# Four changes of order in a two-layer mixer and FFN trunk: splits of block sums, turns of the values, PSUM-emptying steps, and four gate pairs

## The chip, the core and the metric

The kernel runs on one core of a Trainium2 chip. The metric is the device time of one execution in microseconds (us). Engines are named as the profile does: PE (TensorE matmuls, PEld its weight loads), DVE (VectorE), ACT (ScalarE), POOL (GpSimd), SP (SyncE, which here only issues DMAs).

## What is computed

Two layers on x of 1024 tokens by 1024, all in float32. Each layer norms x, projects it with one matrix w_in (1024 by 5120) to queries, keys and values of two attentions and to two gates, runs both attentions, joins them by the gates, projects with w_o and adds to x. A gated FFN with a short convolution follows. The part of the reference that matters here:

```python
proj = h @ w_in[l]
qa, ka, va, qb, kb, vb, gate_pre = jnp.split(proj, splits, axis=-1)
o_a = dilated_mixture(hd4(qa, DSW_HEADS), hd4(ka, DSW_HEADS), hd4(va, DSW_HEADS))
o_b = stick_breaking_attention(hd4(qb, SB_HEADS), hd4(kb, SB_HEADS), hd4(vb, SB_HEADS))
gates = jax.nn.sigmoid(gate_pre + b_gate[l])
merged = g_a * (o_a @ w_br[l, :OUT_A]) + g_b * (o_b @ w_br[l, OUT_A:])
x = x + merged @ w_o[l]
```

The dilated mixture has three groups of four heads with dilations 1, 4 and 16; the stick-breaking attention has four heads.

## The kernel before

**Numbers.** Each float32 operand is split into a high and a low part of type fp32r (`split`, L142 and L147: a cast on ACT, then a subtraction on DVE), and a product is three matmuls: high by high, high by low and low by high.

**A layer's mixer.** `head(l)` first projects the values (`v_ps`) and the keys and queries (`kq_ps`, `q_ps`) of the first heads of the stick-breaking attention. Each PSUM bank is emptied by a step on ACT and one on DVE (L557 and L558 for values, L582/L583 and L579/L580 for keys and queries in `in_parts`), and the parts go to DRAM.

The rest of the input projection is a list of work that the class `Dense` hands out in *shares* (a share is six matmuls of 128x512 in the products of pairs). There are four plain gates (`gate`, tile `g_ps`), and then *pairs*: two column blocks of w_in at once, by seven products in place of eight (Strassen's method, function `pair`, L1055 to L1120). The products are gathered in PSUM banks `i_a`, `i_c`, `i_a`, `i_c`, `i_a`, `i_b`, `i_a`; each is emptied by a step of ACT or DVE (L1087, 1091, 1094, 1100, 1105, 1112, and the last in `put`, L1119). A pair is 14 shares. The right-hand sides include sums of blocks of h: S[1] to S[4], built by `block_sums` (L980 on): sums on POOL (L990, 995, 996, tile `h_sum`, three instructions each), and splits of these into `t_hi` on ACT and `t_lo` on DVE by `in_two`. S[3], the first series of sums, is read by the fifth product of a pair. `series` hands the steps out one at a time while the head's products run (`dense.aside`).

Pairs are of four kinds: `pair_near` (keys and queries of near heads), `pair_v` (values, which are transposed by PE in `turn` (`v_t`, L1161) into a buffer `vv` and written to DRAM as `tv`), `pair_kq` (keys and queries of the far groups, written to DRAM as `tk0` and `tk1` for the two pairs of heads, L1134), and `pair_gate`. Before, a layer's order (`dense.main`, then `dense.seven`) is: near 2, v 0, near 4, near 6, v 1, kq 1 0, kq 2 0, v 2, kq 1 1, kq 2 1, and then the six gate pairs 2 to 7.

**Attention between the shares.** `attend` writes the items of both attentions between the shares: 16 stick items (B), 4 near items (N) and 16 far items (T00 to T07 for `tk0`, T10 to T17 for `tk1`). A far item fetches keys and queries from DRAM (`fetch_kq`, L834, tile `t_kq`, 768 KB), computes scores `z` (L621, L622) at least LEAD_T = 3 shares later, transposes (`t`, L881 to L883), splits (`p1h`, `p1l`) and applies them (`o`, L891, L893). Fetches of T1x need the pairs kq 1 1 and kq 2 1 done, those of T0x kq 1 0 and kq 2 0. A first stick item has a mask on DVE (L685), a scan, and an output `sb_o` (L725) of the split `sbl`.

**What sets the order.** PE's order is that of the code. The order on ACT, DVE and POOL is the Tile scheduler's, which goes by its model of the times, by priorities, and by dependencies added by hand; `tc.high_priority(offset=AHEAD)` with AHEAD = 200 puts a step ahead of others, and a NO_SYNC dependency orders two instructions of one engine without a semaphore. SP issues DMAs in program order, and an issue that has to wait for its data holds up those behind it.

Of the kernel before, what the change touches and what calls it, by code (L numbers as in the profile page):

```python
# [12 lines left out]
ALU = mybir.AluOpType  # L13
# [6 lines left out]
KD = D // P  # L20
# [7 lines left out]
SCALE = 0.125  # L28
# [16 lines left out]
RATE_N = 0.75  # L45
RATE_T = 0.5
PLAIN = 4
LEAD = 6
LEAD_N = 7
LEAD_T = 3  # L50
# [2 lines left out]
AHEAD = 200  # L53
# [3 lines left out]
def f32(ap):  # L57
    return ap.bitcast(F32)
# [3 lines left out]
def trunk_kernel(ctx, tc, x, norm1, w_in, b_gate, w_br, w_o, norm2, w_up, conv_w, conv_b, w_down, norm_f, out, depth=None, probe=None):  # L62
# [23 lines left out]
    LAST = {}  # L86
# [49 lines left out]
        return sb.tile([P, 2048 // c, c], dtype, tag="xa", bufs=4, name=name)  # L136


    def split(hi, lo, src, turn=None):


        one = act.copy(hi, src)  # L142
        if turn == "is":
            LAST["act"] = one.ins.name
        elif turn == "waits" and "act" in LAST:
            tc.add_manual_dep(one.ins, LAST["act"], NO_SYNC, reason="in turn")
        two = dve.tensor_tensor(lo, src, f32(hi), ALU.subtract)  # L147
        if turn == "is":
            LAST["dve"] = two.ins.name
        return two  # L150
# [390 lines left out]
    def values_part(vt, w, ms):  # L541
        for m in ms:
            o = bank("ps", "v_ps")
            for j in range(2):
                t = 2 * m + j
                n, c = t // 4, t % 4
                tok = slice(c * P, (c + 1) * P)
                pairs = []
                for k in range(KD):
                    hh, hl = h_part(n, k)  # L550
                    pairs.append(((hh[:, tok], hl[:, tok]), w[k]))
                yield from product(o[:, j * 256 : (j + 1) * 256], pairs)
                if j == 0:
                    yield
            ov = o.rearrange("p (j h c) -> p j h c", j=2, h=4)
            vv = vt[m // 2][:, 2 * (m % 2) : 2 * (m % 2) + 2, :, :]
            act.copy(vv[:, :, :, 0:64], ov)  # L557
            dve.tensor_tensor(vv[:, :, :, 64:128], ov, f32(vv[:, :, :, 0:64]), ALU.subtract)  # L558
# [17 lines left out]

    def in_parts(c, scale, hi, lo, x):
        if c:
            act.mul(hi, x, scale)  # L579
            dve.scalar_tensor_tensor(lo, x, scale, f32(hi), ALU.mult, ALU.subtract)  # L580
        else:
            act.copy(hi, x)  # L582
            dve.tensor_tensor(lo, x, f32(hi), ALU.subtract)  # L583

    def kq_half(c, w, n):
        o = bank("ps", "kq_ps"[c:])
        yield from product(o, [(w[k], h_part(n, k)) for k in range(KD)])
        hi, lo = small("kq_h", F32R), small("kq_l", F32R)
        in_parts(c, SCALE, hi, lo, o)
        keep_kq(c, n, 0, hi, lo)  # L590
        yield

# [387 lines left out]
    def block_sums(more):  # L980


        last, rs = {}, {}

        def first(t, a, b, i):
            if i == 0:
                new_s(t)
                rs[t] = quarter("h_sum") if t == 3 else sb.tile([P, 4, HF], F32, tag="ql", bufs=2, name="h_sum")
            r, (ah, al), (bh, bl) = rs[t][:, i, :], a()[i], b()[i]
            one = pool.tensor_tensor(r, f32(al), f32(bl), ALU.subtract)  # L990
            if last:
# [4 lines left out]
            last["sum"] = pool.tensor_tensor(r, r, f32(bh), ALU.subtract).ins.name  # L996

        def second(i):
            if i == 0:
                new_s(2)  # L1000
            in_two(1, i)
            r, (ah, al) = rs[1][:, i, :], b22()[i]
            dve.tensor_tensor(r, f32(ah), r, ALU.subtract)
            dve.tensor_tensor(r, r, f32(al), ALU.add)

        def fourth(i):
            if i == 0:
                S[4] = half(0, 0)
            r, (ah, al) = small("h_sum"), b21()[i]
            dve.tensor_tensor(r, f32(ah), f32(S[2][i][0]), ALU.subtract)  # L1010
            dve.tensor_tensor(r, r, f32(S[2][i][1]), ALU.subtract)
            dve.tensor_tensor(r, r, f32(al), ALU.add)
            split(*S[4][i], r, "waits")

        def in_two(t, i):
            split(*S[t][i], rs[3 if t == 3 else 1][:, i, :], "waits")

        b11, b12, b21, b22 = (lambda n=n, k=k: half(n, k) for k in range(2) for n in (1, 0))
        todo = []

        def series(after, lag, gap, f, g):

            at = {}
            for i in range(4):
                at.setdefault(i * gap, []).append(lambda i=i: f(i))
                at.setdefault(i * gap + lag, []).append(lambda i=i: g(i))
            for k in range(3 * gap + lag + 1):
                todo.append((after, lambda fs=at.get(k, ()): [h() for h in fs]))

        series(set(), 3, 2, lambda i: first(3, b22, b12, i), lambda i: in_two(3, i))  # L1030
        series({"head"}, 3, 2, lambda i: first(1, b12, b11, i), second)
        for i in range(4):
# [15 lines left out]
    def pair(dense, l, offs, tiled, put):  # L1048
# [35 lines left out]
        pa, pc = bank("ps", "i_a"), bank("ps", "i_c")  # L1084
        yield from seven(pa, w1, half(1, 0), True, True)
        yield
        act.copy(view(u1), grid(pa))  # L1087
        w7 = piece(u2, "waits")
        yield from seven(pc, w5, S[1], True, True)
        yield  # L1090
        act.copy(view(u5), grid(pc))
        w2 = piece(a12)
        yield from seven(pa, w6, S[2], False, True)
        act.copy(view(u2), grid(pa))
# [5 lines left out]
        dve.tensor_tensor(view(u2), view(u2), grid(pc), ALU.add)  # L1100
# [4 lines left out]
        dve.tensor_tensor(view(u5), view(u5), grid(pa), ALU.add)  # L1105
# [6 lines left out]
        dve.tensor_tensor(view(u1), view(u1), grid(pb), ALU.add)  # L1112
        put(0, 1, u1, False, a12)
        yield
        yield "turn"
        for word in seven(pa, w4, S[4], False, True):
            yield
            yield "turn"
        put(1, 1, grid(pa), True)  # L1119
        yield  # L1120

    def pair_kq(dense, l, g, pr):
# [32 lines left out]
    def pair_v(dense, l, g):  # L1155


        def turn(c, n, f):
            tp = bank("s", "v_t")
            for r in range(4):  # L1160
                pe.transpose(tp[:, r * P : (r + 1) * P], f[:, r * P : (r + 1) * P], ident)  # L1161
            tw = tp.rearrange("p (r h c) -> p r h c", r=4, h=2)
            vv = sb.tile([P, 4, 2, P], F32R, tag="ot", name="vv")
            with tc.high_priority(offset=AHEAD):
                act.copy(vv[:, :, :, 0:64], tw)
                dve.tensor_tensor(vv[:, :, :, 64:128], tw, f32(vv[:, :, :, 0:64]), ALU.subtract)
            for h in range(2):
                if g:
                    there = tv[c][h, :, :, g - 1, n * P : (n + 1) * P].rearrange("r p c -> p r c")
                else:  # L1170
                    there = sv[4 + 2 * c + h][:, 4 * n : 4 * n + 4, :]
                nc.sync.dma_start(there, f32(vv[:, :, h, :]))
            if (c, n) == (1, 1):
                dense.done |= {f"v{g}"} if g else {f"V{u}" for u in range(4, 8)}

        def put(c, n, x, psum, room=None):
            f = x
            if psum:
                f = small("vf")
                act.copy(f.rearrange("p (r j) -> p r j", r=4) if g else f, x)  # L1180
            dense.at(3, lambda: turn(c, n, f))

        off = OFF_VA + 256 * g
        return pair(dense, l, (off, off + P), g > 0, put)
# [34 lines left out]
    def mixer(l, pending):  # L1219
# [1 line left out]
        vectors = setup(l)  # L1221
        dense = Dense()
        dense.plain = [gate(l, c) for c in range(PLAIN)]
        dense.seven = [pair_gate(dense, l, e) for e in range(PLAIN // 2, KD)]
        dense.side = block_sums([(set(), zeros)] * (l == 0))
        dense.done |= {"K0", "K1", "V0", "V1", "V2", "V3"}
        if l:
# [25 lines left out]
        for _ in vectors:  # L1253
            pass
        dense.main = [
            *((None, set(), f, True) for f in (pair_near(dense, l, 2), pair_v(dense, l, 0), pair_near(dense, l, 4), pair_near(dense, l, 6))),
            *((None, set(), f, True) for f in (pair_v(dense, l, 1), pair_kq(dense, l, 1, 0), pair_kq(dense, l, 2, 0))),
            *((None, set(), f, True) for f in (pair_v(dense, l, 2), pair_kq(dense, l, 1, 1), pair_kq(dense, l, 2, 1))),
        ]
# [816 lines left out]
```

## Times and profile before

| what | value |
|---|---|
| median of 3 runs | 2702.91 us (2699.21 to 2703.39) |
| profiled execution | 2701.9 us, span 2700.0 us |
| mean granted clock of PE | 0.992 |
| PE busy | 2635.3 us, 98% of the span |
| DVE, ACT, POOL busy | 2084.5, 1342.1, 673.6 us |

One execution was profiled; rows give start and duration in us. In a wait row, "A <- B: s, n, m" says that A's engine was idle n times before it, s us together and m at most, and that B ended this. Rows with `xN` group N instructions. Issues on SP are told apart from the landing of the DMA they start, which the page lists as "DMA to landing".

### The profile page before, as it was taken

The page shows a single profiled execution, that of the slowest core. Times are in us where ns is not written, and L with a number is a line of the kernel's source. Part 1 is how long each engine was busy: PE and PEld are TensorE (multiplying, and loading weights), DVE is VectorE, ACT ScalarE, POOL GpSimd, SP SyncE. Part 2 cuts the span into 40 slices and gives each one's busy share as a digit, 9 for nine tenths or more (in the row PEclk, how much of TensorE's full clock was granted, in tenths as well). Part 3 has the DMA queues.
Part 4 walks back from the last instruction along what each step waited for, and adds up shares of the span by engine and source line. Part 5 has one row for each costly group of instructions (what it writes and reads, how often), then busy time and mean ns, then how long its engine had stood idle before and what let it go on. Part 6 is the DMA issues. An engine that isn't in the chain of part 4 may idle for free.

```text
span 2700.0 us, 36777 instructions
## 1 busy us (share of the span) xinstructions
PE 2635.3 (98%) x12780; PEld 2201.9 (82%) x12780; DVE 2084.5 (77%) x3159; ACT 1342.1 (50%) x2488; POOL 673.6 (25%) x483
## 2 busy tenths in 40 slices
PE   8899999999999999999989999999999999999999
PEld 7778788888888888888877787888888888888888
DVE  5687776786789888897657778667858888988865
ACT  5355555565555555432334555655745545454225
POOL 5200011112224433321161011010321443343210
PEclk9999999999999999999999999999999999999999
DMA  6546566674335443588443565856732444446863
GB/s 214 171 131 172 152 189 195 220 257 134 90 117 170 139 160 136 214 326 313 173 117 115 154 161 153 234 191 211 265 87 78 154 158 138 167 144 254 328 251 122
DMA packets 418917, 482.94 MB, mean 179 GB/s; under 512 B 26420, under 2 KB 336044, under 8 KB 416940
## 3 DMA queue, kind: packets, MB, share of 16 engines
q1 hardware_dynamic: 418716, 480.59, 55.4%
q8 instruction: 101, 1.65, 0.3%
q14 instruction: 84, 0.69, 0.1%
q10 hardware_dynamic: 16, 0.00, 0.0%
HBM read 307.43 MB, written 173.08 MB: 178 GB/s over the span
## 4 chain that ended last, share of the span: by engine, by line
PE 81%; DVE 9%; ACT 2%; DMA 2%; issue 2%; POOL 1%; SPq 0%; DVEq 0%; ACTq 0%; POOLq 0%
PE u_a L974 5%; PE u_a L975 5%; PE u_a L976 5%; PE d_ps L1704 4%; PE d_ps L1705 4%; PE d_ps L1706 4%; PE i_a L974 3%; PE i_a L976 3%; PE i_a L975 3%; PE u_c L974 3%; PE u_c L976 3%; PE u_c L975 3%; PE o_ps L179 2%; PE o_ps L181 2%; PE o_ps L180 2%; PE i_c L974 2%
## 5 line engine op out<-in xcount | busy, mean ns | idle before, releaser
L147 DVE TENSOR_TENSOR w_lo<-up_a,w_hi 128x512 fp32r<-128x512 f32 x240 | 237.5, 996 | 20.7 <-ACT w_hi L142 20.7
L142 ACT CAST w_hi<-up_a 128x512 fp32r<-128x512 f32 x240 | 149.4, 622 | 184.4 <-PE u_a L975 45.3
L1070 POOL TENSOR_TENSOR u<-in_a 128x512 f32<-128x512 f32 x32 | 45.2, 1412 | 767.0 <-DMA in_a<-in_w_in_dram 232.8
L1712 DVE TENSOR_TENSOR x<-x,d_ps 128x512 f32<-128x512 f32 (+1 forms) x228 | 152.1, 671 | 78.0 <-PE d_ps L1706 76.9
L1443 POOL TENSOR_TENSOR cv<-cv 128x512 f32<-128x512 f32 x88 | 132.3, 1516 | 249.2 <-DVE cv L1438 126.3
L142 ACT CAST w_hi<-in_a 128x512 fp32r<-128x512 f32 x192 | 119.3, 621 | 124.2 <-PE i_c L975 39.0
L147 DVE TENSOR_TENSOR w_lo<-in_a,w_hi 128x512 fp32r<-128x512 f32 x192 | 139.8, 728 | 36.0 <-ACT w_hi L142 33.3
L147 DVE TENSOR_TENSOR g<-cv,g 128x512 fp32r<-128x512 f32 x154 | 152.0, 988 | 5.2 <-ACT g L142 2.7
L1704 PE MATMUL d_ps<-gd_in,w_hi 128*128 128x512 f32 (+1 forms) x340 | 130.3, 383 | 1.4 <-ACT w_hi L142 0.6
L1706 PE MATMUL d_ps<-gd_in,w_lo 128*128 128x512 f32 (+1 forms) x340 | 129.8, 382 | 0.0
L1705 PE MATMUL d_ps<-gd_in,w_hi 128*128 128x512 f32 (+1 forms) x340 | 129.7, 382 | 0.0
L974 PE MATMUL u_a<-hh,w_hi 128*128 128x512 f32 x320 | 124.7, 390 | 0.9 <-DVE u L1594 0.9
L974 PE MATMUL u_a<-t_hi,w_hi 128*128 128x512 f32 x320 | 124.5, 389 | 0.0
L976 PE MATMUL u_a<-t_hi,w_lo 128*128 128x512 f32 x320 | 124.5, 389 | 0.0
L976 PE MATMUL u_a<-hh,w_lo 128*128 128x512 f32 x320 | 124.5, 389 | 0.0
L975 PE MATMUL u_a<-hl,w_hi 128*128 128x512 f32 x320 | 124.5, 389 | 0.0
L975 PE MATMUL u_a<-t_lo,w_hi 128*128 128x512 f32 x320 | 124.5, 389 | 0.0
L147 DVE TENSOR_TENSOR w_lo<-w_raw,w_hi 128x512 fp32r<-128x512 f32 x96 | 74.7, 782 | 58.9 <-ACT w_hi L142 54.8
L142 ACT CAST g<-cv 128x512 fp32r<-128x512 f32 x154 | 94.9, 617 | 40.4 <-POOL cv L1443 29.8
L1704 PE MATMUL d_ps<-gd_in,wd 128*128 128x512 f32 (+1 forms) x292 | 113.9, 390 | 0.0
L1706 PE MATMUL d_ps<-gd_in,wd 128*128 128x512 f32 (+1 forms) x292 | 112.8, 386 | 0.0
L1705 PE MATMUL d_ps<-gd_in,wd 128*128 128x512 f32 (+1 forms) x292 | 112.7, 386 | 0.0
(397 smaller groups left out, 8545.3 us busy)
## 6 DMA issues: line engine op xcount, KB each, us to landing
gd<-g SPq DMA_DIRECT2D x154, 512.0 KB, 3.7
gd_in<-gd SPq DMA_DIRECT2D x154, 512.0 KB, 6.1
up_a<-in_w_up_dram SPq DMA_DIRECT2D x80, 512.0 KB, 5.3
in_a<-in_w_in_dram SPq DMA_DIRECT2D x64, 512.0 KB, 5.5
t_kq<-tk SPq DMA_DIRECT2D x32, 768.0 KB, 4.3
wd_raw<-in_w_down_dram SPq DMA_DIRECT2D x22, 1024.0 KB, 11.7
gin<-gs SPq DMA_DIRECT2D x32, 512.0 KB, 4.3
w_raw<-in_w_o_dram SPq DMA_DIRECT2D x64, 256.0 KB, 2.9
```

The source lines that it names most:

```text
L142: one = act.copy(hi, src)
L147: two = dve.tensor_tensor(lo, src, f32(hi), ALU.subtract)
L179: pe.matmul(o, lh, rh, start=(first and i == 0), stop=False, skip_group_check=share)
L180: pe.matmul(o, lh, rl, start=False, stop=False, skip_group_check=share)
L974: pe.matmul(o, w[0][:, c], rh, start=(first and i == 0), stop=False, skip_group_check=True)
L975: pe.matmul(o, w[0][:, c], rl, start=False, stop=False, skip_group_check=True)
L976: pe.matmul(o, w[1][:, c], rh, start=False, stop=(last and i == 3), skip_group_check=True)
L1443: return lambda: pool.tensor_tensor(dst, a, b, ALU.subtract)
L1704: pe.matmul(o[:, sub], wh[:, c], gh[:, sub], start=(i == 0 and k in (0, 4, 5)), stop=False, skip_group_check=True)
L1705: pe.matmul(o[:, sub], wh[:, c], gl[:, sub], start=False, stop=False, skip_group_check=True)
L1706: pe.matmul(o[:, sub], wl[:, c], gh[:, sub], start=False, stop=(i == m - 1), skip_group_check=True)
L1712: dve.tensor_tensor(x, x, o[:, sub], ALU.add)
```

## The change

There are four parts.

1. `split` gets an argument `behind`, a pair of instructions, and its steps on ACT and DVE are ordered behind them without a semaphore. `in_two` gives `LAST["head"]`, the pair of steps that emptied the head's PSUM bank last (set in `values_part` and in `kq_half`). For S[3], `todo` is no longer a series of sums and splits: the four sums come first, and the four splits follow when the head is done.
2. The turn of a value block comes 5 shares after its product, before 3.
3. The steps that empty a pair's PSUM banks run at high priority, offset AHEAD = 200.
4. EARLY = 4: four of the six gate pairs move from the end of the list (`dense.seven`) to `dense.main`, between near 2 and v 0. The gate pairs 6 and 7 stay at the end. So in shares counted from the layer's start, kq 1 1 ends at 213 (157 before), kq 2 1 at 227 (171), kq 1 0 at 171 (115), v 2's turns lie at 198 to 204 (140 to 146). T02's scores are at 216 in both, T10's at 230 before and 231 after.

```diff
+EARLY = 4
...
-    def split(hi, lo, src, turn=None):
+    def split(hi, lo, src, turn=None, behind=None):
         one = act.copy(hi, src)
+        if behind:
+            tc.add_manual_dep(one.ins, behind[0], NO_SYNC, reason="behind")
...
         two = dve.tensor_tensor(lo, src, f32(hi), ALU.subtract)
+        if behind:
+            tc.add_manual_dep(two.ins, behind[1], NO_SYNC, reason="behind")
...
+            LAST["head"] = one.ins.name, two.ins.name
...
-        in_parts(c, SCALE, hi, lo, o)
+        LAST["head"] = in_parts(c, SCALE, hi, lo, o)
...
-            split(*S[t][i], rs[3 if t == 3 else 1][:, i, :], "waits")
+            split(*S[t][i], rs[3 if t == 3 else 1][:, i, :], "waits", LAST["head"])
...
-        series(set(), 3, 2, lambda i: first(3, b22, b12, i), lambda i: in_two(3, i))
+        for i in range(4):
+            todo.append((set(), lambda i=i: first(3, b22, b12, i)))
+        for i in range(4):
+            todo.append(({"head"}, lambda i=i: in_two(3, i)))
...
-        act.copy(view(u1), grid(pa))
+        with tc.high_priority(offset=AHEAD):
+            act.copy(view(u1), grid(pa))
...
-        put(1, 1, grid(pa), True)
+        with tc.high_priority(offset=AHEAD):
+            put(1, 1, grid(pa), True)
...
-            dense.at(3, lambda: turn(c, n, f))
+            dense.at(5, lambda: turn(c, n, f))
...
-        dense.seven = [pair_gate(dense, l, e) for e in range(PLAIN // 2, KD)]
+        gates = [pair_gate(dense, l, e) for e in range(PLAIN // 2, KD)]
+        dense.seven = gates[EARLY:]
...
-            *((None, set(), f, True) for f in (pair_near(dense, l, 2), pair_v(dense, l, 0), pair_near(dense, l, 4), pair_near(dense, l, 6))),
+            *((None, set(), f, True) for f in (pair_near(dense, l, 2), *gates[:EARLY], pair_v(dense, l, 0), pair_near(dense, l, 4), pair_near(dense, l, 6))),
```

**The order, where it changes.** Numbers behind a name tell buffers apart. First DVE in the head of layer 0, before: `kq_l` and `vb` empty PSUM banks, `t_lo` are splits of sums, `w_lo` of a plain gate's weights.

```order
L580 SCALAR_TENSOR_TENSOR kq_l_679<-q_ps_647,kq_h_678 128x512
L147 TENSOR_TENSOR t_lo_667<-h_sum_668,t_hi_666 128x512 x2
L558 TENSOR_TENSOR vb_229<-v_ps_688,vb_229 128x8x64
L147 TENSOR_TENSOR t_lo_667<-h_sum_668,t_hi_666 128x512 x2
L147 TENSOR_TENSOR t_lo_910<-h_sum_911,t_hi_909 128x512
L147 TENSOR_TENSOR w_lo_918<-w_raw_915,w_hi_917 128x512
L147 TENSOR_TENSOR w_lo_924<-w_raw_921,w_hi_923 128x512
L1003 TENSOR_TENSOR h_sum_911<-hh0_207,h_sum_911 128x512
L558 TENSOR_TENSOR vb_229<-v_ps_749,vb_229 128x8x64
```

After, the same place (line numbers of the changed kernel: L586 and L589 for L580 and L583, L563 for L558, L150 for L147), from the second `vb` on:

```order
L563 TENSOR_TENSOR vb_229<-v_ps_748,vb_229 128x8x64
L150 TENSOR_TENSOR w_lo_918<-w_raw_915,w_hi_917 128x512
L150 TENSOR_TENSOR w_lo_924<-w_raw_921,w_hi_923 128x512
L589 TENSOR_TENSOR kq_l_829<-kq_ps_803,kq_h_828 128x512
L2065 COPY g2_81<-pt_c_871 128x8
L2065 COPY bg_82<-pt_c_871 128x16
L2065 COPY cw_83<-pt_c_871 128x66
L586 SCALAR_TENSOR_TENSOR kq_l_862<-q_ps_836,kq_h_861 128x512
L2065 COPY cb_84<-pt_c_871 128x22
L2065 COPY g1_80<-pt_c_871 128x8
L150 TENSOR_TENSOR t_lo_667<-h_sum_668,t_hi_666 128x512 x4
```

All four `t_lo` of S[3] now stand behind the head's last `kq_l`.

The second place is DVE in layer 0's first pair, where the first stick item lies. Before, from the mask on `z` to `sbl`:

```order
L685 TENSOR_TENSOR z_1384<-z_1384,mask_b_77 128x128
L1011 TENSOR_TENSOR h_sum_1353<-h_sum_1353,t_lo_962 128x512
L147 TENSOR_TENSOR hl0_208<-h_sum_1328,hh0_207 128x512
L1012 TENSOR_TENSOR h_sum_1353<-h_sum_1353,hl1_459 128x512
L1075 TENSOR_TENSOR in_a_1305<-in_a_1305 128x512
L147 TENSOR_TENSOR w_lo_1367<-in_a_1305,w_hi_1366 128x512
L147 TENSOR_TENSOR hl0_208<-h_sum_1353,hh0_207 128x512
L147 TENSOR_TENSOR w_lo_1380<-in_a_1305,w_hi_1379 128x512
L700 SCALAR_TENSOR_TENSOR stay_1289<-stay_1289,zero_75 128x512
L1010 TENSOR_TENSOR h_sum_1392<-hh1_458,t_hi_961 128x512
L147 TENSOR_TENSOR sbl_1415<-sb_t_1409,sbh_1414 128x512
```

After:

```order
L692 TENSOR_TENSOR z_1378<-z_1378,mask_b_77 128x128
L1019 TENSOR_TENSOR h_sum_1347<-h_sum_1347,hl1_459 128x512
L1017 TENSOR_TENSOR h_sum_1386<-hh1_458,t_hi_1046 128x512
L707 SCALAR_TENSOR_TENSOR stay_1277<-stay_1277,zero_75 128x512
L150 TENSOR_TENSOR hl0_208<-h_sum_1347,hh0_207 128x512
L150 TENSOR_TENSOR sbl_1409<-sb_t_1403,sbh_1408 128x512
```

`sbl` has four instructions between the mask and itself, where there were nine.

The third place is SP's queue around the far items of layer 0. Before, about the reads of `t_kq` for T02 and T03, there are only writes of gates (`gs`), loads of weights (`in_a`) and of values (`slots`):

```order
L1062 DMA in_a_4908<-in_w_in_dram 128x8x128
L1192 DMA gs_88<-u_4490 128x512
L1062 DMA in_a_4908<-in_w_in_dram 128x8x128
L1192 DMA gs_88<-u5_4658 128x512
L1192 DMA gs_88<-u_4490 128x512
L834 DMA t_kq_4858<-tk0_91 128x1536
L834 DMA t_kq_4893<-tk0_91 128x1536
L1192 DMA gs_88<-gt_4890 128x512
```

After, about the same two reads (L841), and then about those of T10 and T11, which read `tk1`:

```order
L1151 DMA tk1_92<-in_a_4275 64x4x128
L1151 DMA tk1_92<-u_4406 64x4x128
L1151 DMA tk1_92<-kq_h_4859 64x4x128 x2
L1151 DMA tk1_92<-kq_l_4860 64x4x128
L1151 DMA tk1_92<-kq_h_4859 64x4x128 x2
L1151 DMA tk1_92<-kq_l_4860 64x4x128
L841 DMA t_kq_4827<-tk0_91 128x1536
L841 DMA t_kq_4869<-tk0_91 128x1536
```

```order
L1072 DMA in_a_5318<-in_w_in_dram 128x8x128
L1151 DMA tk1_92<-kq_h_5288 64x4x128 x2
L1151 DMA tk1_92<-kq_l_5289 64x4x128
L1151 DMA tk1_92<-kq_h_5288 64x4x128 x2
L1151 DMA tk1_92<-kq_l_5289 64x4x128
L841 DMA t_kq_5298<-tk1_92 128x1536
L841 DMA t_kq_5300<-tk1_92 128x1536
```

The last six writes of a pair (`kq_h` and `kq_l`, which the last product of the pair fills) now stand ahead of the reads.

More of the change, by code (lines that the diff above doesn't have):

```diff
@@ L556, in values_part @@
             vv = vt[m // 2][:, 2 * (m % 2) : 2 * (m % 2) + 2, :, :]
-            act.copy(vv[:, :, :, 0:64], ov)
-            dve.tensor_tensor(vv[:, :, :, 64:128], ov, f32(vv[:, :, :, 0:64]), ALU.subtract)
+            one = act.copy(vv[:, :, :, 0:64], ov)
+            two = dve.tensor_tensor(vv[:, :, :, 64:128], ov, f32(vv[:, :, :, 0:64]), ALU.subtract)
+            LAST["head"] = one.ins.name, two.ins.name
             if m % 2:
@@ L578, in in_parts @@
         if c:
-            act.mul(hi, x, scale)
-            dve.scalar_tensor_tensor(lo, x, scale, f32(hi), ALU.mult, ALU.subtract)
-        else:
-            act.copy(hi, x)
-            dve.tensor_tensor(lo, x, f32(hi), ALU.subtract)
+            one = act.mul(hi, x, scale)
+            two = dve.scalar_tensor_tensor(lo, x, scale, f32(hi), ALU.mult, ALU.subtract)
+        else:
+            one = act.copy(hi, x)
+            two = dve.tensor_tensor(lo, x, f32(hi), ALU.subtract)
+        return one.ins.name, two.ins.name
     def kq_half(c, w, n):
@@ L1090, in pair @@
         yield
[L1091 removed]
+        with tc.high_priority(offset=AHEAD):
+            act.copy(view(u5), grid(pc))
         w2 = piece(a12)
         yield from seven(pa, w6, S[2], False, True)
[L1094 removed]
+        with tc.high_priority(offset=AHEAD):
+            act.copy(view(u2), grid(pa))
         w4 = piece(a22)
@@ L1099, in pair @@
         yield from seven(pc, w3, half(0, 1), False, True)
-        dve.tensor_tensor(view(u2), view(u2), grid(pc), ALU.add)
+        with tc.high_priority(offset=AHEAD):
+            dve.tensor_tensor(view(u2), view(u2), grid(pc), ALU.add)
         put(0, 0, u2, False, a11)
@@ L1104, in pair @@
         yield from seven(pa, w7, S[3], False, True)
-        dve.tensor_tensor(view(u5), view(u5), grid(pa), ALU.add)
+        with tc.high_priority(offset=AHEAD):
+            dve.tensor_tensor(view(u5), view(u5), grid(pa), ALU.add)
         put(1, 0, u5, False, a21)
@@ L1111, in pair @@
         yield from seven(pb, w2, half(1, 1), True, True)
-        dve.tensor_tensor(view(u1), view(u1), grid(pb), ALU.add)
+        with tc.high_priority(offset=AHEAD):
+            dve.tensor_tensor(view(u1), view(u1), grid(pb), ALU.add)
         put(0, 1, u1, False, a12)
@@ L1118, in pair @@
             yield "turn"
-        put(1, 1, grid(pa), True)
+        with tc.high_priority(offset=AHEAD):
+            put(1, 1, grid(pa), True)
         yield
```

## The prediction

> **What bounds the kernel now.** I read the head of the page first: busy times, then the chain that ended last.
>
> ```profile
> span 2700.0 us, 36777 instructions
> PE 2635.3 (98%) x12780; PEld 2201.9 (82%) x12780; DVE 2084.5 (77%) x3159; ACT 1342.1 (50%) x2488; POOL 673.6 (25%) x483
> PE 81%; DVE 9%; ACT 2%; DMA 2%; issue 2%; POOL 1%; SPq 0%; DVEq 0%; ACTq 0%; POOLq 0%
> ```
>
> PE (TensorE) is busy for 98% of the span: 2700.0 - 2635.3 = 64.7 us is all that better waiting can bring, apart from the clock. The change keeps every matmul, in nearly the same order. It can only move PE's waits, so I read the list of waits next, PE's rows alone (sum in us, times, longest).
>
> ```profile
> PE q_ps L179 <- DVE vb L558: 12.0, 1, 12.0
> PE v_ps L179 <- DVE kq_l L583: 7.1, 1, 7.1
> PE v_t L1161 <- DVE u L1100: 5.3, 2, 2.6
> PE sb_o L725 <- DVE sbl L147: 3.9, 2, 2.2
> PE i_c L974 <- DVE kq_l L580: 3.1, 4, 1.3
> PE o L891 <- DVE p1l L147: 2.7, 4, 0.7
> PE v_t L1161 <- DVE vv L1166: 2.2, 2, 1.1
> PE g_ps L179 <- DVE kq_l L583: 2.2, 1, 2.2
> PE i_a L974 <- DVE u L1112: 1.9, 2, 1.0
> PE i_c L974 <- ACT u L1091: 1.6, 1, 1.6
> PE i_a L974 <- DVE u L1105: 1.5, 2, 0.8
> PE kq_ps L179 <- DVE vb L558: 0.6, 1, 0.6
> ```
>
> The two longest belong to the heads. The timeline shows why (start, duration, engine and line; in brackets the idle time before it and what ended that).
>
> ```profile
> 65.20 1.09 DVE L147 TENSOR_TENSOR t_lo<-h_sum,t_hi 128x512 fp32r<-128x512 f32 x1 [3.15 <-ACT t_hi L142]
> 69.11 0.62 ACT L142 CAST t_hi<-h_sum 128x512 fp32r<-128x512 f32 x1 [2.90 <-POOL h_sum L996]
> 71.22 0.68 DVE L558 TENSOR_TENSOR vb<-v_ps,vb 128x512 fp32r<-128x512 f32 x1
> 71.95 0.79 PE L179 MATMUL q_ps<-hh,kq_w 128*128 128x512 f32 x1 [12.04 <-DVE vb L558]
> 75.53 0.40 PE L181 MATMUL q_ps<-hh,kq_w 128*128 128x512 f32 x1
> 82.20 0.69 PE L179 MATMUL g_ps<-hh,w_hi 128*128 128x512 f32 x1 [2.21 <-DVE kq_l L583]
> 1397.72 1.08 DVE L147 TENSOR_TENSOR t_lo<-h_sum,t_hi 128x512 fp32r<-128x512 f32 x1 [3.14 <-ACT t_hi L142]
> 1399.45 0.58 PE L179 MATMUL v_ps<-v_w,hh 128*128 128x256 f32 x1 [7.07 <-DVE kq_l L583]
> ```
>
> PE needs the PSUM bank that `vb` (L558) empties. That step stands on DVE behind a split `t_lo`, which waits for `t_hi` on ACT, which waits for a sum on POOL. It is the order on DVE, not the amount of work. Layer 1 shows the same at 1397.72.
>
> **The change, part by part**, against the profiled execution's own 2701.9 us (span 2700.0).
>
> *Pins of the splits of S[3].* They add no instruction; the splits go from ahead of the head's emptying steps to behind the last of them, on ACT and on DVE. What PE waited there goes: 12.0 + 2.2 + 0.6 in layer 0 and 7.1 in layer 1, together 21.9. After the long waits PE also ran at a longer pace: from 71.95 to 75.53 eight matmuls started, one per 0.45 us, against one per 0.23 in the loaded stretch (483.15 and 483.38 below). That is 8 x 0.22 = 1.8 us, and I count it for each of the three waits over 2 us: 5.3. Sum **-27.2**. Next in line is POOL with its sums. The first product that reads S[3] is the fifth of the first pair, behind four gates and four products, and that work hides the late splits; without it each of the four would cost 0.62 + 1.09 = 1.7 us by the rows of `t_hi` and `t_lo`.
>
> *The first stick item.* The waits for `sbl` are 2.2 (layer 1) and 3.9 - 2.2 = 1.7 (layer 0). In layer 0, nine DVE instructions stood between the mask and `sbl`, and now four; in layer 1 that order stays. I take **-1.7**; the ends are -3.9 and 0.
>
> *Turns of the values two shares later.* `v_t` waits 2.6 us, twice, for the very sum (L1100) that it turns. Two shares are 12 matmuls of 0.23 = 2.8 us of other work, so this wait goes: **-5.3** (it cannot be more). The 2.2 for L1166 are waits for the single buffer `vv`, which a transfer still reads; moving all turns by the same amount leaves them.
>
> *Emptying steps of the pairs.* The waits of `i_a` and `i_c` sum to 3.1 + 1.9 + 1.6 + 1.5 = 8.1. Steps with priority get ahead of weight splits, but still wait for the instruction that runs. Ends 0 and -8.1; I take **-6**, nearer to all of it since one split (0.62 on ACT, 1.09 on DVE) is shorter than most of these waits.
>
> *Four gate pairs early.* The products only change places, 56 shares of them. But the last two pairs of keys and queries, which ended over 40 shares ahead of the first far item, now end inside the far items. Here are the matmuls of before at the places where they will end, the first scores behind each, and the prices of the transfers.
>
> ```profile
> 475.67 2.40 SPq L834 DMA_DIRECT2D t_kq<-tk  x2
> 479.04 0.39 PE L976 MATMUL i_a<-hh,w_lo 128*128 128x512 f32 x1
> 483.15 0.39 PE L975 MATMUL i_a<-hl,w_hi 128*128 128x512 f32 x1
> 483.38 0.40 PE L976 MATMUL i_a<-hh,w_lo 128*128 128x512 f32 x1
> 483.62 0.22 PE L621 MATMUL z<-t_kq 128*128 128x128 f32 x1
> 512.65 0.40 PE L976 MATMUL i_a<-hh,w_lo 128*128 128x512 f32 x1
> 516.38 0.39 PE L891 MATMUL o<-p1l,slots 128*128 128x256 f32 x1 [0.72 <-DVE p1l L147]
> 518.21 0.22 PE L621 MATMUL z<-t_kq 128*128 128x128 f32 x1
> 376.48 0.60 ACT L579 ACTIVATE kq_h<-i_a 128x512 fp32r<-128x512 f32 x1
> L1134 SPq DMA_DIRECT2D tk<-kq_h x32: 574/618/1486, 299.4 to 1735.8; - x32
> DMA to landing us min/median/max: 2.4/2.6/6.1
> DMA to landing us min/median/max: 4.1/4.3/6.1
> tk<-in_a SPq DMA_DIRECT2D x16, 128.0 KB, 3.1
> kv<-sk SPq DMA_DIRECT2D x2, 512.0 KB, 9.5
> ```
>
> (The first landing row is of `tk`'s writes, 2.6, the second of `t_kq`'s reads, 4.3; the last two are the window from 367 to 410 us, in which `tk` was written before.)
>
> The order on SP decides. The pair kq 1 1 ends at the place of 479.04 + 0.39 = 479.4. The read of `t_kq` for the third far item (T02) stands on SP behind that pair's last six writes of `kq_h` and `kq_l`. They wait for the last product and its emptying (0.60, and 0.2 of latency as my estimate: 480.2), take 6 x 0.62 = 3.7 to issue (483.9), and the read lands 4.3 later: 488.2. PE reaches the scores at 483.6. It waits **4.6**. Before, the same read was issued at 475.67. The pair kq 2 1 ends at 513.05. Its six writes stand behind a weight load that needs the room of earlier writes, so they start at about 513.8 and are issued at 517.5; T10's read needs them landed (2.6) and lands itself 4.3 later: 524.4. PE gets to these scores at 518.2, and now later by what the new order has ahead of them, three transposes, four matmuls of `o` and six of 512. The last nine of such a group take from 516.38 to 518.21 = 1.8, so I count 2.1 for all: 520.3. It waits **4.1**. Both are longer than the 2.2 us that was followed by the longer pace at 82.20, so I add 1.8 each. Per layer 4.6 + 4.1 + 3.6 = 12.3, in both **+24.6**. Ends: 0, if the reads come in time after all, and by the landing of 9.5 in the row of `kv` 5.2 more for each of four reads, +45.
>
> *The rest of that move.* Emptying and splitting for eight puts a layer (0.60 on ACT and about 0.7 on DVE each) now falls among the far items, whose `o` already waits 2.7 for `p1l`: I double these, **+2.7** (0 to +5). The turns of the values fall in the near items: one more pair of waits for `vv` at 1.1, **+2.2** (0 to +4).
>
> Sum: -27.2 - 1.7 - 5.3 - 6 + 24.6 + 2.7 + 2.2 = -10.7, so 2701.9 - 10.7 = **2691**. The profiled execution is 1.0 below the median of 2702.91 and inside its runs; I leave it there.
>
> **The pace after a wait, by a page.** PE's rate after a wait is the one price here that hangs on more than order.
>
> ```profile
> 186.21 0.63 PE L1161 MATMUL v_t<-ident,u 128*128 128x128 f32 x4 [2.63 <-DVE u L1100]
> 187.13 0.40 PE L976 MATMUL i_b<-hh,w_lo 128*128 128x512 f32 x1
> 187.37 0.40 PE L974 MATMUL i_b<-hh,w_hi 128*128 128x512 f32 x1
> ```
>
> Here the matmuls came 0.24 apart right after a wait of 2.63, while after the shorter wait of 2.21 (at 82.20) they came at the longer pace. The Trainium skill, "TensorE: Matmul & The Clock Gate", Part 1 (The HAM clock gate), says that the array drops to half rate after an idle window of about 3.4 us, which runs free of the program. The trace agrees that the length of a wait alone does not decide, and disagrees on the threshold, since 2.21 was enough. By that rule a wait of 4.6 covers a whole window in about (4.6 - 3.4) / 3.4, a third, of the cases, and the new waits would mostly cost nothing beyond themselves, an estimate from the page's figure.
>
> **Rivals.**
> 1. *The reads come in time.* If SP or the scores run otherwise than I placed them (both new waits are under 5 us), the +24.6 go: 2691 - 24.6 = 2666. For it: each wait is what is left of a sum of three steps (emptying, issue, landing) against work on PE, and the work could be later by more than I count, since PE's queue then holds other waits. Against: SP issues in order, and the writes' data come last. Chance 0.14.
> 2. *PE stays at its rate after the new waits*, as after 186.21: four times 1.8 less, 2684. For it: that row; against: the pace after 71.95 and after the shorter wait at 82.20. Chance 0.12. The rule of the clock-gate page, above, leads to this case.
> 3. *Slower: the reads collide.* The reads of 768 KB now run beside 20 writes of 128 KB, as the read of `kv` did when it took 9.5 between 367 and 410 us. With 9.5 in place of 4.3 each of four waits is 5.2 longer: 2691 + 20.8 = 2712. It decides from a landing of 4.3 + 10.7 / 4 = 7.0 on. For it: that row. Against: the writes beside it landed in 3.1. Chance 0.17.
> 4. *The pins do not free PE:* half of the head's waits stay, because POOL or ACT is late elsewhere: +13.6, 2705; with no gain from priority, 2711. Against: DVE's order in the head is plain. Chance 0.10.
>
> **How the numbers follow.** The forecast, 2691 with 0.47, has a range of its own from 2682 to 2700 by the ends of the small terms. To reach 8 in 10 I go down to 2667 and up to 2713. A measurement of this kernel tells about 0.2%, 5.4 us, from no change. Of the forecast 0.40 lies below 2696.5; with the first two rivals 0.14 + 0.12 that makes 0.66 faster. Slower (over 2707.3) are 0.16 of the third and 0.04 of the fourth: 0.20. The rest, 0.14, is the same.
>
> **What would show it.** In the changed profile's list of waits the rows of `q_ps` and `v_ps` should be gone or under 1 us; if a row of `h_sum` or S[3]'s splits takes their place, the first part is wrong. `v_t` for L1100 should be gone. The rows of `z` should name a DMA `t_kq<-tk` four times at 4 to 5 us; at 0 the first rival holds, at 9 or more the third. Matmuls 0.43 apart behind these waits tell between the forecast and the second rival. The prediction is wrong if PE's idle sum stays above 64.7 although the heads' rows went, or if waits appear in the parts behind attention, to which I gave nothing.

## The result, and the profile after

| | before | after |
|---|---|---|
| median of 20 runs each, us | 2700.30 (2695.49 to 2704.30) | 2700.81 (2697.51 to 2704.35) |
| span of the profiled execution, us | 2700.0 | 2699.3 |
| mean granted clock of PE | 0.992 | 0.993 |
| PE idle (span less busy), us | 64.7 | 59.7 |

The ratio after to before is 1.0003, with a 95% interval from 0.9997 to 1.0010. The change makes no difference that this measurement can tell. The forecast of 2691 us, a gain of 10.7, was 0.36% too low. The time lies inside the whole range given, 2667 to 2713, but just outside the forecast's own, 2682 to 2700. It is the outcome "the same", which had a chance of 0.14, where "faster" had 0.66.

The head of the page after:

```profile
span 2699.3 us, 36771 instructions
PE 2639.6 (98%) x12780; PEld 2204.6 (82%) x12780; DVE 2083.0 (77%) x3159; ACT 1340.2 (50%) x2488; POOL 676.3 (25%) x483
PE 78%; DVE 12%; DMA 4%; ACT 3%; issue 2%; SPq 0%; POOL 0%; DVEq 0%; ACTq 0%
```

In the chain that ended last, DMA has doubled from 2% to 4% and DVE has risen from 9% to 12%. PE's idle sum fell by 5.0 us, but its busy time rose by 4.3 with the same 12780 matmuls: some of them ran at the longer pace. The list of PE's waits after:

```profile
PE z L628 <- DMA t_kq<-tk: 20.3, 4, 5.7
PE z L628 <- ACT stay L694: 8.8, 8, 3.4
PE z L628 <- DVE vv L1183: 2.7, 2, 1.6
PE j_ps L952 <- DVE on L956: 2.7, 2, 1.3
PE sb_o L732 <- DVE sbl L150: 2.5, 1, 2.5
PE i_c L981 <- ACT gt L1223: 2.0, 1, 2.0
...
PE z L629 <- DMA slots<-sq: 1.5, 2, 0.8
...
PE o_ps L185 <- POOL hl L1342: 1.3, 2, 0.6
PE i_b L981 <- DVE u L1114: 1.2, 2, 0.6
PE o L898 <- DVE p1l L150: 1.2, 4, 0.4
```

The rows of `q_ps`, `v_ps` and `g_ps` (21.3 us before) are gone, and so are those of `v_t`. In their place stands a first row of 20.3 us: PE's scores of far items, waiting four times for the reads of `t_kq`. Smaller rows are new or have grown as well: the scores that wait for `stay` on ACT had 4.0 us in seven waits before and have 8.8 in eight, and `i_c` for `gt` (2.0) and `o_ps` for POOL's `hl` (1.3) had no row before.

Where the time came from and went shows best in the times at which PE first reaches each part (first matmul of the tile named, in us; in brackets the difference from before). The last two columns are experiments told below.

| PE's first matmul of | before | after | e1 (no early gates) | e9 (and writes moved) |
|---|---|---|---|---|
| layer 0, `z` of the first stick item | 94.8 | 76.5 (-18.3) | 77.4 (-17.5) | 76.2 (-18.6) |
| layer 0, `z` of the first far item | 474.3 | 455.4 (-18.9) | 460.8 (-13.5) | 455.6 (-18.7) |
| layer 0, `br_ps` behind attention | 584.7 | 579.6 (-5.1) | 569.8 (-14.9) | 566.0 (-18.7) |
| layer 1, `v_ps` | 1357.6 | 1353.5 (-4.1) | 1343.0 (-14.6) | 1339.2 (-18.4) |
| layer 1, `z` of the first stick item | 1424.5 | 1411.3 (-13.2) | 1400.8 (-23.7) | 1397.1 (-27.4) |
| layer 1, `z` of the first far item | 1803.4 | 1787.4 (-16.0) | 1776.7 (-26.7) | 1771.2 (-32.2) |
| layer 1, `br_ps` behind attention | 1913.8 | 1911.1 (-2.7) | 1887.0 (-26.8) | 1881.6 (-32.1) |
| last row of the kernel | 2693.7 | 2692.9 (-0.8) | 2668.2 (-25.5) | 2663.4 (-30.3) |

So the heads brought 18.3 and 13.2 - 4.1 = 9.1 us, as forecast, and the far items took back 18.9 - 5.1 = 13.8 in layer 0 and 16.0 - 2.7 = 13.3 in layer 1. Between the first stick item and the first far item only 0.6 and 2.8 us were gained.

The place of T02 in layer 0, from ACT's, SP's and PE's timelines after:

```profile
460.54 0.60 ACT L585 ACTIVATE kq_h<-i_a 128x512 fp32r<-128x512 f32 x1
461.16 1.98 SPq L1151 DMA_DIRECT2D tk<-kq_h  x2
465.19 0.62 SPq L1151 DMA_DIRECT2D tk<-kq_l  x1
465.91 1.03 SPq L841 DMA_DIRECT2D t_kq<-tk  x2
470.56 0.47 PE L628 MATMUL z<-t_kq 128*128 128x128 f32 x1 [5.69 <-DMA t_kq<-tk]
473.93 0.63 PE L983 MATMUL i_c<-t_hi,w_lo 128*128 128x512 f32 x1
```

PE came to these scores at 470.56 - 5.69 = 464.87. The read was issued only at 465.91, behind the six writes that had to wait for `kq_h`, and PE began 4.65 us after that. The last row shows that PE is still at the longer pace 3.4 us later (0.63 for a matmul that takes 0.40 in the loaded stretch). T10 shows the same chain, with the landing of a write in it. The first and the fourth row are from the chain of work in the window from 500 to 515 us; by it the read was issued only when a write of `kq_l` had landed:

```profile
504.94 3.57 DMA tk<-kq_l
506.90 0.63 SPq L1151 DMA_DIRECT2D tk<-kq_l  x1
508.57 0.80 SPq L841 DMA_DIRECT2D t_kq<-tk  x2
508.57 4.83 DMA t_kq<-tk
513.44 0.48 PE L628 MATMUL z<-t_kq 128*128 128x128 f32 x1 [4.63 <-DMA t_kq<-tk]
```

### The profile page after: what moved, and what is told of

Read it like the earlier page. It is cut to its first block, busy times and chain, and to the rows that moved or that the text cites. A ratio compares the mean times of both kernels' runs of the same rounds, so it can differ in the third digit from the quotient of the medians.

```text
span 2699.3 us, 36771 instructions
## 1 busy us (share of the span) xinstructions
PE 2639.6 (98%) x12780; PEld 2204.6 (82%) x12780; DVE 2083.0 (77%) x3159; ACT 1340.2 (50%) x2488; POOL 676.3 (25%) x483
## 4 chain that ended last, share of the span: by engine, by line
PE 78%; DVE 12%; DMA 4%; ACT 3%; issue 2%; SPq 0%; POOL 0%; DVEq 0%; ACTq 0%
PE u_a L981 5%; PE u_a L983 5%; PE u_a L982 5%; PE d_ps L1722 5%; PE d_ps L1724 4%; PE d_ps L1723 4%; PE i_a L981 3%; PE i_a L983 3%; PE i_a L982 3%; PE u_c L983 2%; PE u_c L982 2%; PE u_c L981 2%; PE o_ps L184 2%; PE o_ps L185 2%; PE o_ps L186 2%
## 5 line engine op out<-in xcount | busy, mean ns | idle before, releaser
L150 DVE TENSOR_TENSOR w_lo<-up_a,w_hi 128x512 fp32r<-128x512 f32 x240 | 237.5, 996 | 20.5 <-ACT w_hi L143 20.4
L150 DVE TENSOR_TENSOR w_lo<-in_a,w_hi 128x512 fp32r<-128x512 f32 x192 | 136.9, 714 | 37.6 <-ACT w_hi L143 33.6
L150 DVE TENSOR_TENSOR g<-cv,g 128x512 fp32r<-128x512 f32 x154 | 152.0, 988 | 5.2 <-ACT g L143 2.7
L150 DVE TENSOR_TENSOR w_lo<-w_raw,w_hi 128x512 fp32r<-128x512 f32 x96 | 76.7, 803 | 49.6 <-ACT w_hi L143 49.4
L143 ACT CAST g<-cv 128x512 fp32r<-128x512 f32 x154 | 94.9, 616 | 40.0 <-POOL cv L1461 29.6
L1722 PE MATMUL d_ps<-gd_in,wd 128*128 128x512 f32 (+1 forms) x292 | 113.9, 390 | 0.0
L707 DVE TENSOR_TENSOR_SCAN stay<-stay,zero 128x512 f32<-128x512 f32 (+2 forms) x96 | 100.4, 1056 | 16.6 <-ACT stay L694 16.4
L1724 PE MATMUL d_ps<-gd_in,wd 128*128 128x512 f32 (+1 forms) x292 | 112.8, 386 | 0.0
```

The source lines that it names most:

```text
L707: one = dve.tensor_tensor_scan(rev, rev, zero[:, 0:1].to_broadcast([P, c1 - c0]), 1.0 if c1 == L else sv[:, c1 : c1 + 1], ALU.mult, ALU.add)
L1722: pe.matmul(o[:, sub], wh[:, c], gh[:, sub], start=(i == 0 and k in (0, 4, 5)), stop=False, skip_group_check=True)
L1724: pe.matmul(o[:, sub], wl[:, c], gh[:, sub], start=False, stop=(i == m - 1), skip_group_check=True)
```

## Experiments

Times are medians. Each ratio is to the kernel of before on the same chip, so the medians of before differ a little between groups (2698.8, 2701.7, 2701.9 and 2700.3 us). The theory was the prediction's sum: early gates cost what PE waits for the far reads, and the other parts bring the rest. The main rival was that waits only change places.

**e1: no early gates.**

```diff
-EARLY = 4
+EARLY = 0
```

> The changed kernel with EARLY = 0, so the gate pairs stay last and only the pins, the turns and the priorities remain. Theory A (the early gates cost what PE waits at the reads of t_kq, 20.3 us in four waits, and the slower matmuls behind them, 4 x 2.3 = 9.3): 2700.8 - 29.6 = 2671 us, 0.989 of before, and no row of z waiting for t_kq. Rival B (the waits at the reads only take up time that DVE needs anyway, and other waits grow when they go): 2690 us or more, 0.996, with longer waits of o, j_ps or z in the far items.

Measured: 2677.2 us, ratio 0.9920 (0.9907 to 0.9932). It lies between the two. The rows of `t_kq` are gone, but a new one has come:

```profile
PE z L628 <- DMA kv<-sk: 5.3, 2, 2.7
```

It has the same cause at another place. With early gates gone, the pair kq 1 0 ends where a stick item reads its keys (`kv`):

```profile
286.75 0.63 SPq L1151 DMA_DIRECT2D tk<-kq_l  x1
287.42 0.63 SPq L1151 DMA_DIRECT2D tk<-u  x1
288.15 0.55 SPq L657 DMA_DIRECT2D kv<-sk  x1
```

PE was at the scores at 288.36 (it began at 291.01 after 2.65 idle), the read was issued at 288.15, behind the pair's writes. So early gates cost about 22 us net. They take 20.3 of waits and four times 2.3 of longer pace (29.6 together). Against that they keep kq 1 0 away from the stick items, whose waits for `kv` cost e1 5.3 and some 1.9 of longer pace; 29.6 - 7.2 = 22.4.

**e2: the six last writes of the pair kq 1 1 behind the reads.**

```diff
-            for s in range(2):
-                ...
+            def write():
+                for s in range(2):
+                    ...
+            if psum and (g, pr) == (1, 1):
+                dense.at(2, write)
+            else:
+                write()
```

> The changed kernel, but the last six writes of the pair kq 1 1 are issued two shares later, behind the reads of t_kq for T02 and T03. Theory A (the read for T02 is late because it stands behind these writes on SP): the waits of 5.7 and 5.1 at T02 go with 2.3 each of slower matmuls, 2700.8 - 15.4 = 2685 us, 0.994 of before; the waits at T10, 4.6 and 4.9, stay. Rival C (the read is late because the writes and reads share the DMA engines): T02 still waits 3 us or more, 2695 to 2701.

Measured: 2691.8 us, 0.9971 (0.9959 to 0.9982). Half of the expected gain. In layer 0 the read now is issued at 460.10 in place of 465.91, and T02's wait falls from 5.69 to 1.28; but T03, whose read is issued with it, now waits as well:

```profile
460.10 2.51 SPq L841 DMA_DIRECT2D t_kq<-tk  x2
```

```profile
465.26 0.33 PE L628 MATMUL z<-t_kq 128*128 128x128 f32 x1 [1.28 <-DMA t_kq<-tk]
477.60 0.30 PE L628 MATMUL z<-t_kq 128*128 128x128 f32 x1 [1.35 <-DMA t_kq<-tk]
```

SP's order therefore is most of it (5.69 - 1.28 = 4.4 us at T02). The rest fits rival C, though no run tests it alone: in the window from 455 to 480 us the reads' median landing is 6.2 us in e2, against 4.3 after. In layer 1 T02 still waits 2.12, where it waited 5.06.

**e3 and e4: the pins alone, and the early gates alone,** on the kernel of before.

> The kernel of before with the pins of the splits of S[3] alone. Theory A: 21.9 us of waits and three times 1.8 of slower matmuls go, but DVE's splits of the gates' weights now run beside POOL's sums and take 1.7 us each in place of 0.7, which lengthens the wait of the first stick scores from 1.6 to 3.4 and adds 1.7 of slower matmuls: -27.2 + 3.5 = -23.7, 2676.6 us, 0.991. Rival D (the wait only moves to POOL's sums): 2690 or more.

> The kernel of before with the four gate pairs early alone. Theory A: the four waits at the reads of t_kq with their slower matmuls, 20.3 + 9.3 = 29.6 us, less the waits that go behind them: 2700.3 + 29.6 = 2730 us, 1.011. Rival B (they take up time that is needed anyway): 2710 or less, 1.004.

Measured: pins alone 2678.4 us, 0.9922 (0.9910 to 0.9934); early gates alone 2722.3 us, 1.0076 (1.0061 to 1.0090). The pins came out as theory A had them; the early gates lie between the two theories (2730 and 2710). They cost 20.5 us without the other parts and 22.4 with them (1.0003 less 0.9920), so within the intervals the parts add up. Partly this is chance: by PE's first matmuls the far items lost 10.9 + 10.0 us in e4 and 13.8 + 13.3 after, while the `kv` waits that early gates avoid come only with the priorities (e1 and e6 have them, e3 and e7 do not). Two rows of e4 show the head's wait untouched and the far reads:

```profile
PE z L622 <- DMA t_kq<-tk: 16.7, 6, 5.8
PE q_ps L180 <- DVE vb L559: 12.1, 1, 12.1
```

**e5: two gate pairs early.**

```diff
-EARLY = 4
+EARLY = 2
```

> The changed kernel with EARLY = 2, so kq 1 1 and kq 2 1 end at shares 185 and 199, ahead of the first far scores at 212. Theory A (only reads that stand behind the writes of an unfinished pair cost): no wait of z for t_kq over 2 us, 2677 to 2683 us, 0.992 to 0.994. Rival B2 (each early gate pair costs its part of 23.6, because attention then runs beside more of the work of ACT and DVE): 2677.2 + 11.8 = 2689 us, 0.996.

Measured: 2712.4 us, 1.0041 (1.0029 to 1.0053). Both theories missed, by 30 and 23 us. No row for `t_kq` is left, as A had it, but scores of stick items now wait elsewhere: 18.3 us for `stay`, where e1 has 8.4, and still 4.4 in two for reads of `kv`. The row of the list comes first, then POOL's, DVE's and PE's timelines at the longest of these waits:

```profile
PE z L628 <- ACT stay L694: 18.3, 8, 5.4
```

```profile
236.38 1.89 DVE L707 TENSOR_TENSOR_SCAN stay<-stay,zero 128x512 f32<-128x512 f32 x1
237.27 2.06 POOL L1081 TENSOR_TENSOR in_a<-in_a 128x512 f32<-128x512 f32 x1
238.20 1.68 DVE L150 TENSOR_TENSOR w_lo<-in_a,w_hi 128x512 fp32r<-128x512 f32 x1
239.80 0.28 DVE L692 TENSOR_TENSOR z<-z,mask_b 128x128 f32<-128x128 f32 x1
241.75 0.58 PE L628 MATMUL z<-kv,slots 128*128 128x256 f32 x1 [5.45 <-ACT stay L694]
```

The mask that PE's next scores wait for stands on DVE behind a scan and a weight split, and both run beside POOL's sums for a pair's weights. There are two waits of this kind, and several of about 2 us that are followed by the longer pace. Against e1, PE's idle sum is 20.1 us larger (62.7 and 42.6) and its busy time 19.1 us (2651.0 and 2631.9), with the same matmuls. That says where the loss lies; why this order of pairs meets these waits and EARLY = 0 and 4 do not stays open.

**e6 and e7: the priorities and the later turns, one at a time,** each with the pins, without early gates. In e6 the turns are back at 3; in e7 the `high_priority` lines are gone.

> The changed kernel with EARLY = 0 and the turns at 3 again: pins and priorities. Against the pins alone (2678.4 us): by the waits of i_a and i_c, 3.0 + 2.0 + 1.4 + 0.8 = 7.2 there, the prediction's term is -5, 2673. Rival E (what PE gains it loses at the next read of keys, which lands no sooner): 2678, with a row of z for kv<-sk.

> The changed kernel with EARLY = 0 and without the priorities: pins and the later turns. Against the pins alone (2678.4 us): the prediction's term is -5.3 and the slower matmuls behind one of the two waits -1.7, 2671.5 us. Rival E (lost again at the next read of keys): 2678.

Measured: pins and priorities 2687.0 us, 0.9951 (0.9939 to 0.9963); pins and turns 2677.4 us, 0.9916 (0.9903 to 0.9929). With pins alone at 0.9922 and all three (e1) at 0.9920, neither part gains alone: the priorities lose 8 us (2687.0 is also 9 us above rival E's 2678), and the turns stay within the interval. The turns have the time of rival E but not its cause, since e7 has no row of `kv<-sk`. The row that answers the prediction's step on the turns is this one of e7:

```profile
PE i_b L981 <- DVE u L1110: 5.1, 2, 2.5
```

The wait for the sum that `v_t` had waited for is still there, two times 2.5 us. It has only passed to the product `i_b` behind it. In e6 these rows are new against the pins, or a little larger (the third was 2.6):

```profile
PE z L628 <- DMA kv<-sk: 5.4, 2, 2.8
...
PE v_t L1178 <- ACT stay L694: 3.4, 2, 1.7
PE v_t L1178 <- DVE vv L1183: 2.7, 2, 1.5
```

The read of keys (rival E) is one of them. It does not account for all of e6's loss, for which the list of waits has no single cause; PE's idle sum is 7.7 us above that of e3 (53.3 and 45.6). The cause stays open.

**e8: stick items' scores two shares later** (LEAD = 8, EARLY = 0).

> The changed kernel with EARLY = 0 and LEAD = 8 in place of 6, so that every stick item's scores come two shares later behind the read of their keys. Theory A (the waits of z for kv<-sk, 5.3 us in two, and 1.9 of slower matmuls come from that read standing behind the writes of a pair on SP, and two shares of 1.4 cover them): 2677.2 - 7 = 2670 us, 0.989. Rival F (two shares later the scores meet another wait, on ACT or DVE): 2677 or more.

Measured: 2701.7 us, 1.0001 (0.9993 to 1.0010). Rival F, and far beyond it: the row of `kv<-sk` is gone, but LEAD moves every stick item, and others come in its place. Against e1 PE is idle 11.6 us longer (54.2 and 42.6) and busy 15.0 us longer (2646.9 and 2631.9).

```profile
PE o L898 <- ACT p1h L143: 4.5, 4, 2.0
...
PE z L628 <- DMA slots<-sq: 4.0, 2, 3.0
```

**e9: the last writes of every far pair two shares later,** EARLY = 0 (the edit of e2 with `if psum:`). This touches SP's order only.

> The changed kernel with EARLY = 0, and the last six writes of every pair of keys and queries of the far groups issued two shares later, so that the read of a stick item's keys (kv) goes ahead of them on SP. Theory A (SP's order is what holds the reads back): the waits of z for kv<-sk, 2.7 twice, and 1.6 of slower matmuls behind one of them go: 2677.2 - 7 = 2670 us, 0.989. Rival G (the keys land late by the transfers beside them): within 2 us of 2677.

Measured: 2671.2 us, 0.9885 (0.9863 to 0.9906), as theory A had it, and the best of all versions with the full sums. No row of `kv<-sk` is left. Against e1 that is 6.0 us by the medians and 0.0035, or 9 us, by the ratios.

**e10: short sums on POOL.** EARLY = 0.

```diff
-            pool.tensor_tensor(r, r, f32(ah), ALU.add)
-            last["sum"] = pool.tensor_tensor(r, r, f32(bh), ALU.subtract).ins.name
+            last["sum"] = one.ins.name
```

> The changed kernel with EARLY = 0, and each of POOL's eight block sums a layer cut to the first of its three instructions: two block terms are left out of S[1] and S[3], so this is for timing alone. Theory H (the first stick scores of layer 0 wait 3.4 us because DVE's instructions beside POOL's sums take 1.5 to 1.7 us in place of 0.7): the gates' weight splits there take 0.7 each, and that wait falls to 1.6 or less. Rival I (the wait comes from the order on DVE alone): it stays over 2.5.

Measured: one run, 2674.3 us. The first scores of layer 0 wait 1.57 us, the value of before, where e1, which differs from e10 in the sums alone, has 3.43. First the rows after, then those of e10, and last the wait of before:

```profile
77.06 1.62 POOL L1002 TENSOR_TENSOR h_sum<-h_sum,hh 128x512 f32<-128x512 f32 x1
77.45 3.45 DVE L150 TENSOR_TENSOR w_lo<-w_raw,w_hi 128x512 fp32r<-128x512 f32 x2
82.28 0.50 PE L628 MATMUL z<-kv,slots 128*128 128x512 f32 x1 [3.42 <-ACT stay L694]
```

```profile
73.66 0.69 DVE L150 TENSOR_TENSOR w_lo<-w_raw,w_hi 128x512 fp32r<-128x512 f32 x1 [3.23 <-ACT w_hi L143]
79.67 0.50 PE L628 MATMUL z<-kv,slots 128*128 128x512 f32 x1 [1.57 <-ACT stay L694]
```

```profile
98.73 0.50 PE L621 MATMUL z<-kv,slots 128*128 128x512 f32 x1 [1.57 <-ACT stay L687]
```

Theory H holds: beside POOL a split took 3.45 / 2 = 1.73 us, alone 0.69. The pins bring gates and sums side by side, which they were not before.

**e11: e9 without the priorities.**

> As the run with the last six writes of the far pairs two shares later (EARLY = 0, 2671.2 us), but without the priorities of the emptying steps. Theory J (the priorities gain about 6 us, which the later reads of keys took back until the writes were moved): pins and turns had no waits for those reads, so moving the writes gives nothing here: 2677, 0.991, and the priorities are worth 6 us beside the moved writes. Rival K (moving the writes is worth 6 us by itself, the priorities nothing): 2671, 0.989.

Measured: 2676.3 us, 0.9906 (0.9890 to 0.9923), near theory J's 2677. With the writes moved, the priorities seem worth about 5 us (2676.3 to 2671.2), but the intervals of e9 and e11 overlap from 0.9890 to 0.9906, so this size is not clear of noise. The lists of waits agree with it: `i_b` for `u` has 5.1 us in e11 and 0.6 in e9, and the waits of `i_c` for `kq_l` (3.1 in e11) have no row in e9. Without the moved writes (e7 to e1) the priorities were worth nothing, and e1 has 5.3 us of waits for `kv` that e7 does not have.

## Why the prediction was right or wrong

**The heads: right.** Forecast 18.4 in layer 0 and 8.9 in layer 1, measured 18.3 and 9.1 at the first stick scores.

**The far items: right in mechanism, and nearly in size.** Forecast: waits of 4.6 at T02 and 4.1 at T10 in each layer, and in fact 20.3 / 4 = 5.1 on average. The longer pace behind each cost 2.3 (pitch of the matmuls behind them) and not 1.8. Together 20.3 + 9.3 = 29.6, against 24.6. By the table the far items lost 13.8 + 13.3 = 27.1, against 24.6 + 2.7 with the puts. That the sums agree so well is luck: the waits were dearer, and the term for the puts had the wrong sign, since the waits of `o` fell from 2.7 to 1.2 and those of `j_ps` from 3.9 to 2.7. The extra waits for `vv` (+2.2) did not come either: before they have 2.2, after 2.7. The 0.2 of latency in T02's sum is shown by no row; after, the chain has 0.02 between the last product and `kq_h`, and the first write starts 0.02 after `kq_h`. The first rival (reads in time) is out. So is the third (reads landing at 9.5): the median landing of T02's window stayed 4.3. The second, that PE keeps its rate behind these waits, is out by the row at 473.93. The Trainium skill, "TensorE: Matmul & The Clock Gate", Part 1 (The HAM clock gate), gives an idle window of about 3.4 us that runs free of the program; by it a part of these four waits should have cost nothing more. All four, of 4.6 to 5.7 us, were followed by the longer pace, with 2.3 us lost behind each, and at another place a wait of only 2.02 was too (the last section), so here the measurement decides against that reading.

**The step that failed: "so this wait goes" for the turns, and "I take -6" for the emptying steps.** Together they stood for 11.3 us and brought 1.2 by the medians (e3 to e1), within the noise. For the turns alone, e7 shows the wait passing to `i_b`, whose first matmul comes right behind the transposes and needs the same step: I had asked what waits, and not who waits next for the same thing. With the priorities as well (e1) the waits that both terms named do go: of 5.3 + 8.1 = 13.4 us before, 2.9 are left in the rows of `i_a`, `i_b` and `i_c`. But the time was not gained: PE now waits 5.3 us for reads of keys that SP's order holds back, and e9, which moves only the writes, brings 6.0. What the priorities alone add to that (e11) is not clear of noise.

**Mis-sized: the pins.** They were forecast at 27.2; alone they bring 0.0078 of 2698.8 = 21 us, or 23.6 by the spans of the profiled executions. The heads gave all of it, but the first scores of layer 0 then waited 3.42 us in place of 1.57 (4.41 in e3), behind weight splits beside POOL's sums. The longer pace behind that wait cost 1.4 more: the tenth matmul starts 3.58 us after the first, and 2.18 in e10. I had called these sums hidden since their results come early enough, and had not asked what they do to the work beside them. The stick item's term was 1.7; after, one wait of 2.5 us stands in layer 1 in place of 1.7 and 2.2. A second new wait behind the heads is that of `i_c` for `gt`, 2.02 at 129.45. Every run with the pins has it and before does not; no experiment was made on it.

**What is left.** The parts behind attention, to which I gave nothing, lost 2.9 us after (from -5.1 to -4.1 between `br_ps` and the next layer, and from -2.7 to -0.8 up to the end), and 1.6 in e1. The prediction had named waits there as a sign of being wrong, and there are some: `o_ps` for POOL's `hl`, 1.3 us, which before does not have, and `d_ps` for `w_hi`, 1.2 in place of 0.6. No experiment was made on that, and the cause stays open.

By parts, the forecast was -27.2 - 1.7 for pins and stick item, -11.3 for turns and emptying steps, and +29.5 for the early gates (24.6 + 2.7 + 2.2), together -10.7. By the ratios the runs gave -21.1 (e3), -0.5 (e1 against e3) and +22.4 (after against e1), together +0.8. These steps end at the result by the way they are formed; what they show is the sizes. The two gains were sized too high by 18.6, and the loss too high by 7.1. So the sum missed by 11.5 and the forecast gain did not come; that the time still lies in the whole range is owed to errors of opposite sign and to the room given to the rivals.

## What to carry to other kernels

When a wait is taken away, look for the next instruction that needs the same step or the same queue: here two waits of 2.6 us only passed to the matmul behind them, and what was gained at PSUM went into two reads that stood behind writes. On a queue that issues in order, a write whose data come late holds back every read behind it; putting the last six writes of each far pair two shares later was worth 6 us, while moving the readers (e8) brought other waits and lost 24.5. When a block of equal work is moved, check what ends late because of it, and price each transfer that follows its last result.

## What the runs showed of the hardware

A TENSOR_TENSOR on DVE and one on POOL slowed each other here. `w_lo` of 128x512 took 0.69 us alone and 1.73 beside POOL's sums (e10 and after, above); a scan took 1.22 alone (after, at 82.26) and 1.89 beside POOL in e5. POOL's sums took 1.28 alone and 1.62 to 1.82 beside DVE, by these rows after:

```profile
62.70 1.28 POOL L1002 TENSOR_TENSOR h_sum<-h_sum,hh 128x512 f32<-128x512 f32 x1
66.68 1.82 POOL L1002 TENSOR_TENSOR h_sum<-h_sum,hh 128x512 f32<-128x512 f32 x1
75.24 1.74 POOL L997 TENSOR_TENSOR h_sum<-hl,hl 128x512 f32<-128x512 f32 x1
75.86 1.66 DVE L1011 TENSOR_TENSOR h_sum<-h_sum,hl 128x512 f32<-128x512 f32 x1
```

The Trainium skill, "SBUF — State Buffer", section "Who interferes with whom", says that DVE with two SBUF inputs and POOL share one pair of ports, which one instruction holds while the other waits. The trace agrees in kind: both engines take about 1.7 us an instruction there, somewhat below the sum of their times alone, 0.69 + 1.28 = 1.97. The forecast left this out; it was worth about 3.2 us in the first scores of layer 0 (1.85 of wait and 1.4 of longer pace).

The pace behind a wait was not set by its length alone. The same wait of 2.02 us at the same matmul of `i_c` was followed by a granted clock of 0.56 after (from 131.0 to 134.4 us) and of 1.00 in e1 (130.2 to 134.0). From that matmul to the next product's first (`i_a`) it took 4.92 us after and 3.36 in e1.
